# Down projection of a two-layer trunk: Winograd's seven products in another order, their row sums made one layer step earlier

## The chip, the cores and the metric

The kernel runs on one core of a Trainium2 chip. The metric is the device time of one execution in microseconds (us). TensorE (PE) multiplies, VectorE (DVE) and ScalarE (ACT) prepare its operands and empty its accumulators, SyncE (SP) issues all large transfers from one queue in order.

## The reference, cut to what matters

Two layers on 1024 tokens of width 1024. The first mixes tokens by sparse attention, the second by a short gated convolution; each is followed by a feed-forward block of hidden width 2816 and a scaled addition to the residual stream x.

```python
def _swiglu(h, w_gate, w_up, w_down):
    return (jax.nn.silu(h @ w_gate) * (h @ w_up)) @ w_down

def reference(x, c, ...):
    c_act = jax.nn.silu(c)
    for i in range(DEPTH):
        mod = c_act @ ada_w[i] + ada_b[i]
        sh1, sc1, g1, sh2, sc2, g2 = [m[:, None, :] for m in jnp.split(mod, 6, axis=-1)]
        h = _rmsnorm(x, norm1_g[i]) * (1.0 + sc1) + sh1
        ...
        x = x + g1 * y
        h = _rmsnorm(x, norm2_g[i]) * (1.0 + sc2) + sh2
        x = x + g2 * _swiglu(h, ffn_w_gate[i], ffn_w_up[i], ffn_w_down[i])
    return x
```

The change concerns the last product, the down projection `... @ w_down`, and what stands around it.

## The kernel before, in words

Everything is held with the features on the 128 partitions and 512 tokens (one half of the sequence) along the free dimension, so a tile is 128x512 in float32. A float32 product is made of three fast ones: `split` writes a rounded copy `hi` (a CAST on ACT) and the rest `lo` (a subtraction on DVE) of each operand, and `mm3` multiplies hi by hi, hi by lo and lo by hi.

The large products use Winograd's variant of Strassen: both operands are cut into 2x2 blocks, and seven products of sums of blocks take the place of eight. The weights' sums are S1 to S4, the activations' sums are T1 to T4, and M1 to M7 are the products. M1 takes two blocks as they are, M6 takes S2 and T2, M5 takes S1 and T1, M7 takes S3 and T3, M3 takes S4 and one block, M4 takes one block and T4, M2 two blocks.

`Tail` holds the code from the first feed-forward block to the end. It runs `ffn` (layer 0), `down_pairs`, `conv`, `down`, `ffn` (layer 1), `down_pairs`. In `ffn` a set is 256 hidden features: a `Pair` of weight columns for the gate and one for up, seven products each (84 matmuls of 512 columns). `norm_second` forms the second half's operands at the start of `ffn` and of `conv`; meanwhile the first two products of the first `EARLY` = 8 pairs, which need the first half alone, are made (`Pair.early`), and what does not fit is put away in DRAM (`Pair.put`, `Pair.get`). The hidden rows go to DRAM (`hidden`). `side_steps` does eight steps per set of the second layer's modulation, one DVE multiply-add (`adacc`) each.

`down_pairs` sums over 11 steps p of 256 hidden features, and takes four passes over them: M1 and M2 in one, M6 and M5, M7 and M3, and M4 alone. A product of one step is 12 matmuls into four PSUM banks, so a pass of two products holds all eight banks (tags mm, g and sm) and the next pass needs them empty. T1, T2, T3 and T4 are formed by DVE inside the passes from rows that the first pass fetches. In the fourth pass the generator `between` runs the next norm (`norm_first`) or the stores of the output (`store`).

The order on each engine is not written by hand: each operation is recorded, and `Plan.drain` issues them by a cost model, on each engine the earliest recorded of those that are ready. The result is a fixed order on each engine. All instructions are issued from one helper, so that every row of the profile has line L244; tiles tell them apart. In `down_pairs` the tiles named ph hold weights and operands there, rt, rh and cv hold rows, whi and wlo are the operands from the ring of `unit`, u and v are scratch, xr is x, raw are loaded weights.

Of the kernel before, what the change touches and what calls it, by code (L numbers as in the profile page):

```python
# [450 lines left out]
P = 128  # L451
# [900 lines left out]
class Tail:  # L1352
# [4 lines left out]
    EARLY, KEPT, SIDE = 8, 4, 4  # L1357
# [3 lines left out]
    def __init__(self, tk, ada_w, xspill):  # L1361
        self.tk, self.nc, self.plan, self.ada_w = tk, tk.nc, tk.plan, ada_w
        plan = tk.plan
        plan.pri = None
        xp = Pool(plan, "x2")
        self.up = Pool(plan, "u", bufs=6)
        self.bp = Pool(plan, "h2")
        self.tp = Pool(plan, "t2")
        self.sp = Pool(plan, "s2", bufs=4)
        self.first = (xp, self.up, self.bp)  # L1370
        self.second = (self.tp, self.sp)
        xr = xp.tile([P, KT, T], F32, name="xr")
# [3 lines left out]
        self.hid = [[plan.wrap(plan.tc.dram_tile([P, HW], F32, name="hid%d_%d" % (i, f)), [P, HW])  # L1376
                     for f in range(FT)] for i in range(NH)]
# [164 lines left out]
    def down_pairs(self, w, layer, j, between):  # L1542
# [4 lines left out]
        order = range(FT // 2)  # L1547
        hi, raw = (self.bp.tile([P, 8, HW], t, name="p" + v, tag=v)
                   for v, t in zip(self.FIRST, (F32R, F32)))
        b, loads, units = {}, [], []  # L1550
        x = lambda i, k, d: (1 - k, 4 * i + d)

        def rows(p):
            if p in b:
                return b[p]
            if p == 0:
                b[p] = [self.cv() for _ in range(4)]
            else:
                name = self.SECOND[(p - 1) // 2]
                t = self.tp.tile([P, 8, HW], F32, name="r" + name, tag=name)  # L1560
                for i in range(2):
                    b[p + i] = [t.part_of(4 * i + v)[:, 4 * i + v] for v in range(4)]
            return b[p]

        def fetch(p, k):
            for i in range(2):
                nc.sync.dma_start(rows(p)[2 * k + i], self.hid[1 - k][2 * p + i])

        def load(p, half):
            i = len(loads) % 4 * 2  # L1570
            loads.append(raw.part_of(i)[:, i:i + 2])
            nc.sync.dma_start(loads[-1], w[2 * p * P:(2 * p + 2) * P, half_of(half)].rearrange(
                "(j p) n -> p j n", p=P))
            return loads[-1][:, 0], loads[-1][:, 1]
# [6 lines left out]
        def total(x, y, op, s=None):  # L1581
            s = self.s4() if s is None else s
            tt(s, x, y, op)
            return s

        def products(ps, p, *ab):
            for bank, (a, c) in zip(ps, ab):
                (ahi, alo), (chi, clo) = tk.unit(), tk.unit() if len(ps) == 1 else unit()
                self.tk.split(a, ahi, alo)
                self.tk.split(c, chi, clo)  # L1590
                for d in range(4):
                    tk.mm3(bank[d], ahi[:, blk(d)], alo[:, blk(d)], chi, clo,
                           p == order[0], p == order[-1])

        def banks():
            return [[tk.ps("sm") if (i, d) == (0, 3) else self.bank() for d in range(4)]
                    for i in range(2)]

        def add_to(ps, i, k, d):
            self.add(ps, layer, j, *x(i, k, d))  # L1600

        ps = banks()
        for n, p in enumerate(order):
            fetch(p, 0)
            products(ps, p, *zip(load(p, 0), rows(p)[0:2]))
            if n:
                fetch(order[n - 1], 1)
        fetch(order[-1], 1)
        u = [self.u() for _ in range(4)]
        for d in range(4):  # L1610
            self.plan.copy(u[d], ps[0][d])
        for d in range(4):
            add_to(ps[1][d], 0, 0, d)
            add_to(u[d], 0, 0, d)
        ps = banks()
        for p in order:
            b11, b21, b12, b22 = rows(p)
            a21, a22 = load(p, 1)
            s1 = total(a21, a22, add)
            a11 = tk.load(w[blk(2 * p), half_of(0)])  # L1620
            s2 = total(s1, a11, sub)
            t1 = total(b12, b11, sub)
            total(b22, t1, sub, b11)
            products(ps, p, (s2, b11), (s1, t1))
        for d in range(4):
            nc.vector.tensor_tensor(u[d], u[d], ps[0][d], op=add)
        for d in range(4):
            v = self.v()
            nc.vector.tensor_tensor(v, u[d], ps[1][d], op=add)
            add_to(v, 0, 1, d)  # L1630
            add_to(v, 1, 1, d)
            add_to(u[d], 1, 0, d)
        ps = banks()
        for p in order:
            b11, b21, b12, b22 = rows(p)
            (a11, a12), (a21, a22) = (load(p, i) for i in range(2))
            s3 = total(a11, a21, sub)
            t3 = total(b22, b12, sub)
            s4 = total(s3, a22, sub)
            total(s4, a12, add, s4)  # L1640
            products(ps, p, (s3, t3), (s4, b22))
        for d in range(4):
            add_to(ps[0][d], 1, 1, d)
            add_to(ps[0][d], 1, 0, d)
        for d in range(4):
            add_to(ps[1][d], 0, 1, d)
        ps = [[tk.ps("g") for _ in range(4)]]
        for p in order:
            next(between, None)
            b11, b21, b12, b22 = rows(p)  # L1650
            a22 = tk.load(w[blk(2 * p + 1), half_of(1)])
            products(ps, p, (a22, total(b21, b11, sub)))
        for _ in between:
            pass
        for d in range(4):
            add_to(ps[0][d], 1, 0, d)


    def ffn(self, layer, w_gate, w_up):
        sets = [(Pair(self, w_gate, f), Pair(self, w_up, f)) for f in range(0, FF, 2 * P)]  # L1660
        self.norm_second(layer, 1, [p for s in sets for p in s][:self.EARLY])
        for f, (gate, up) in enumerate(sets):
# [6 lines left out]
            for i, row in enumerate(up.done()):  # L1669
# [33 lines left out]
    def run(self, w_gate, w_up, w_down, w_in, w_out, out):  # L1703
        self.side = [(1, j, i, k) for j in range(1, 6) for i in range(NH) for k in range(KT)]
        self.ffn(0, w_gate[0], w_up[0])
        self.down_pairs(w_down[0], 0, 5, self.norm_first(1, 0))
# [3 lines left out]
        self.down_pairs(w_down[1], 1, 5, (self.store(out, half, d) for half, n in ((0, KT), (1, 4))  # L1710
                                          for d in range(n)))
        for d in range(4, KT):
            self.store(out, 1, d)

    def store(self, out, half, d):
        ps, o = self.tk.ps(), self.u()
# [111 lines left out]
```

## Time and profile before

| | |
|---|---|
| time, median of 3 runs | 2344.18 us (2337.61 to 6151.19) |
| the profiled execution | 2345.58 us, span 2343.9 us |
| PE busy | 2262.7 us (97%), 11742 matmuls |
| DVE busy | 1901.5 us (81%) |
| ACT busy | 1109.5 us (47%) |
| moved by DMA | 312.32 MB, 133 GB/s over the span |

The share of the span in which an engine had an instruction in it is averaged over stages. On PE the recorded matmuls overlap, so what it does not do is read from its waits and from the distance of the starts.

### The profile page before, as it was taken

The numbers are of one execution on the slowest core, as the hardware profiler recorded it, in microseconds if no ns is written. First come the engines' busy times: TensorE is split into PE (matmuls) and PEld (weight loads), VectorE is DVE, ScalarE is ACT, GpSimd is POOL, SyncE is SP. The second block draws the span as 40 slices with busy tenths as digits, with TensorE's granted clock in tenths as the row PEclk, the third lists the DMA queues.
The fourth block names the chain that finished last, engine by engine and source line by source line (L and its number), as shares of the span: only waits on it lengthen the run. The fifth ranks groups of instructions, "written<-read, shape, count | busy, mean of one in ns | idle before, by whom it ended". The sixth has DMA issues, their size and how long they took to land.

```text
span 2343.9 us, 32878 instructions
## 1 busy us (share of the span) xinstructions
PE 2262.7 (97%) x11742; PEld 1830.8 (78%) x11742; DVE 1901.5 (81%) x3848; ACT 1109.5 (47%) x2109; POOL 5.6 (0%) x19
## 2 busy tenths in 40 slices
PE   6999999999999999999999899999999999999999
PEld 6657876876797888888887677788878888888877
DVE  6879999777679888878599989886898766666996
ACT  3576899846655333333343552223553333334434
POOL 0000000000000000000000000000000000000000
PEclk7999999999999999999999999999999999999999
DMA  8424243433334554444844144334344322238343
GB/s 286 133 63 89 89 120 95 132 122 104 118 118 139 175 171 135 135 135 138 326 144 151 58 128 126 90 90 157 109 121 146 97 90 77 90 118 313 126 162 113
DMA packets 305134, 312.32 MB, mean 133 GB/s; under 512 B 15145, under 2 KB 209738, under 8 KB 304970
## 3 DMA queue, kind: packets, MB, share of 16 engines
q1 hardware_dynamic: 303530, 308.91, 42.2%
q8 instruction: 92, 1.51, 0.3%
q10 hardware_dynamic: 1440, 1.31, 0.2%
q14 instruction: 72, 0.59, 0.1%
HBM read 259.05 MB, written 51.12 MB: 132 GB/s over the span
## 4 chain that ended last, share of the span: by engine, by line
PE 71%; DVE 15%; issue 7%; DMA 5%; ACT 2%; POOL 0%; SPq 0%; DVEq 0%; ACTq 0%; POOLq 0%
PE ps_g L244 39%; PE ps_mm L244 23%; PE ps_sm L244 5%; DVE u L244 2%; PE ps_L L244 2%; DVE wlo L244 2%; PE ps_o L244 2%; DVE s L244 2%; DVE v L244 2%; DVE p L244 1%; DVE xr L244 1%; DVE sc L244 1%; DMA raw<-in_ffn_w_up_dram 1%; DMA raw<-in_conv_w_in_dram 1%; DMA raw<-in_ffn_w_gate_dram 1%
## 5 line engine op out<-in xcount | busy, mean ns | idle before, releaser
L244 ACT CAST whi<-s 128x512 fp32r<-128x512 f32 x341 | 211.2, 620 | 470.2 <-PE ps_g L244 204.9
L244 PE MATMUL ps_g<-t,whi 128*128 128x512 f32 x1160 | 360.5, 392 | 3.7 <-ACT t L244 3.0
L244 ACT CAST whi<-raw 128x512 fp32r<-128x512 f32 (+1 forms) x283 | 173.0, 618 | 356.6 <-PE ps_g L244 148.4
L244 PE MATMUL ps_g<-h,whi 128*128 128x512 f32 x1080 | 333.7, 390 | 0.0
L244 DVE TENSOR_TENSOR wlo<-raw,whi 128x512 fp32r<-128x512 f32 (+1 forms) x292 | 199.6, 687 | 79.9 <-ACT whi L244 79.3
L244 PEld LDWEIGHTS ps_g<-t,whi 128*128 128x128 f32 x1160 | 218.8, 189 | 51.0 <-ACT t L244 3.4
L244 DVE TENSOR_TENSOR wlo<-s,whi 128x512 fp32r<-128x512 f32 x342 | 234.4, 690 | 23.5 <-ACT whi L244 22.7
L244 PEld LDWEIGHTS ps_g<-h,whi 128*128 128x128 f32 x1080 | 202.1, 188 | 41.5
L244 PE MATMUL ps_g<-t,wlo 128*128 128x512 f32 x580 | 227.4, 392 | 3.9 <-DVE wlo L244 3.9
L244 PE MATMUL ps_g<-h,wlo 128*128 128x512 f32 x540 | 210.6, 390 | 0.3 <-DVE wlo L244 0.3
L244 PE MATMUL ps_g<-ph,whi 128*128 128x512 f32 x660 | 206.5, 392 | 4.2 <-DVE ph L244 2.1
L244 PE MATMUL ps_mm<-t,whi 128*128 128x512 f32 x632 | 197.0, 393 | 3.1 <-ACT whi L244 1.9
L244 PEld LDWEIGHTS ps_g<-ph,whi 128*128 128x128 f32 x660 | 124.9, 189 | 31.2 <-DVE v L244 2.7
L244 PEld LDWEIGHTS ps_mm<-t,whi 128*128 128x128 f32 x632 | 119.8, 190 | 29.2 <-ACT whi L244 2.6
L244 PEld LDWEIGHTS ps_g<-t,wlo 128*128 128x128 f32 x580 | 109.6, 189 | 28.1 <-DVE wlo L244 5.6
L244 PE MATMUL ps_g<-ph,wlo 128*128 128x512 f32 x330 | 129.9, 393 | 0.0
L244 PE MATMUL ps_mm<-t,wlo 128*128 128x512 f32 x316 | 124.2, 393 | 3.3 <-DVE wlo L244 3.3
L244 ACT ACTIVATE p<-p,nm,qsc 128x128 f32<-128x128 f32 (+7 forms) x128 | 112.0, 877 | 27.9 <-DVE nm L244 22.8
L244 DVE CUSTOM_DVE_ANT_0 p<-ps_L,bias 128x512 f32<-128x512 f32 (+3 forms) x192 | 100.1, 553 | 25.3 <-PE ps_sm L244 9.2
L244 PEld LDWEIGHTS ps_g<-h,wlo 128*128 128x128 f32 x540 | 101.4, 188 | 21.9 <-DVE wlo L244 0.8
L244 DVE SCALAR_TENSOR_TENSOR adacc<-adaw,cact,adacc 128x512 f32<-128x512 f32 x140 | 104.8, 748 | 15.6 <-DMA adaw<-in_ada_w_dram 15.3
L244 ACT ACTIVATE junk<-sc,bs 128x896 bf16<-128x896 f32 (+3 forms) x124 | 109.7, 885 | 15.7 <-DVE bs L244 11.1
(334 smaller groups left out, 4738.5 us busy)
## 6 DMA issues: line engine op xcount, KB each, us to landing
ph<-in_ffn_w_down_dram SPq DMA_DIRECT2D x88, 512.0 KB
adaw<-in_ada_w_dram SPq DMA_DIRECT2D x160, 256.0 KB
raw<-in_ffn_w_gate_dram SPq DMA_DIRECT2D x52, 512.0 KB
raw<-in_ffn_w_up_dram SPq DMA_DIRECT2D x52, 512.0 KB
rt<-hid SPq DMA_DIRECT2D x64, 256.0 KB
raw<-in_conv_w_in_dram SPq DMA_DIRECT2D x32, 512.0 KB
hid<-u SPq DMA_DIRECT2D x52, 256.0 KB
raw<-in_ffn_w_down_dram SPq DMA_DIRECT2D x44, 256.0 KB
```

The source lines that it names most:

```text
L244: f(*[a.get() if isinstance(a, Ref) else a for a in args], **{k: a.get() if isinstance(a, Ref) else a for k, a in kw.items()})
```

## The change

It makes T1 to T4 in `ffn`, at the end of each set, and writes seven rows of blocks and sums to DRAM in place of the four hidden rows; `down_pairs` fetches each when a pass needs it. The seven products go in five passes: M1; M6 with M3 one step behind; M5 with M7 one step behind; M2; M4. Each product has four banks, named at each pass. What a finished product adds to x is put on a list and done two entries per step (`later`). `between` runs from the end of the M2 pass on. `EARLY` is 10 in place of 8. One of the five modulation vectors (16 of 80 side steps) moves from the feed-forward block of layer 0 to that of layer 1.

```diff
-    EARLY, KEPT, SIDE = 8, 4, 4
+    EARLY, KEPT, SIDE = 10, 4, 4
...
+        places, loads, units, rest, late = [self.cv() for _ in range(4)], [0], [], [], []
+        for name in ("t4", "t1", "t2", "h22", "t3"):
+            t = self.tp.tile([P, 8, HW], F32, name="r" + name, tag=name)
+            places += [t.part_of(i)[:, i] for i in range(8)]
+        def fetch(p, i, what):
+            nc.sync.dma_start(places[4 * p + i], self.rows[p][what])
...
+        def product(ps, p, a, i, unit=unit):
+            (ahi, alo), (chi, clo) = tk.unit(), unit()
+            tk.split(a, ahi, alo)
+            tk.split(places[4 * p + i], chi, clo)
+            for d in range(4):
+                tk.mm3(ps[d], ahi[:, blk(d)], alo[:, blk(d)], chi, clo, p == 0, p == n - 1)
...
+        def steps(lead, lag=None):
+            for p in range(n):
+                x = lead(p)
+                if late:
+                    f, *a = late.pop()
+                    f(*a)
+                if lag is not None:
+                    late.append((lag, p, x))
+                for f, a in rest[:2]:
+                    f(*a)
+                del rest[:2]
+        def m1(p):
+            fetch(p, 0, "b11")
+            a11, = load(p, 0, 1)
+            product(one, p, a11, 0)
+            fetch(p, 1, "t2")
+        def m6(p):
+            (a11, a12), (a21, a22) = (load(p, i) for i in range(2))
+            tt(a22, a21, a22, add)
+            tt(a22, a22, a11, sub)
+            s4 = self.s4()
+            tt(s4, a12, a22, sub)
+            product(two, p, a22, 1)
+            fetch(p, 2, "b22")
+            fetch(p, 0, "t1")
+            return s4
+        def m3(p, s4):
+            if p == 0:
+                one[:] = banks("g", "g", "g", "sm")
+            product(one, p, s4, 2)
...
+        def m5(p):
+            (a21, a22), (a11,) = load(p, 1), load(p, 0, 1)
+            tt(a22, a21, a22, add)
+            s3 = self.s4()
+            tt(s3, a11, a21, sub)
+            product(two, p, a22, 0)
+            fetch(p, 3, "t3")
+            fetch(p, 1, "b21")
+            return s3
...
+        def m2(p):
+            a12 = tk.load(w[blk(2 * p + 1), half_of(0)])
+            product(two, p, a12, 1, tk.unit)
+            fetch(p, 2, "t4")
+            if p >= start:
+                next(between, None)
+        def m4(p):
+            a22 = tk.load(w[blk(2 * p + 1), half_of(1)])
+            product(one, p, a22, 2, tk.unit)
+            if p >= start - 8:
+                next(between, None)
+        one = banks("g", "g", "g", "sm")
+        steps(m1)
+        u = copies(one, self.u)
+        later(*((add_to, u[d], 0, 0, d) for d in range(4)))
+        two = banks("mm", "g", "mm", "g")
+        steps(m6, m3)
         for d in range(4):
+            nc.vector.tensor_tensor(u[d], u[d], two[d], op=add)
+        later(*((add_to, u[d], 1, 0, d) for d in range(4)))
+        two = banks("mm", "g", "mm", "g")
+        steps(m5, m7)
+        v = copies(two, self.cv)
         for d in range(4):
+            later((tt, v[d], v[d], u[d], add), (add_to, v[d], 0, 1, d), (add_to, v[d], 1, 1, d))
+        two = banks("mm", "g", "mm", "g")
+        steps(m2)
+        add_to(two[0], 0, 0, 0)
+        later(*((add_to, two[d], 0, 0, d) for d in (1, 2, 3)))
+        one = banks("g", "g", "g", "mm")
+        steps(m4)
...
     def ffn(self, layer, w_gate, w_up):
...
-                    self.hidden(2 * f + i, half, t)
+            (b12, b11), (b22, b21) = rows
+            (t2, t1), (t4, _) = gs
+            for t, x, y, op in ((b12, b22, b12, ALU.subtract), (t2, b12, b11, ALU.add),
+                                (t1, b22, t2, ALU.subtract), (t4, b21, t2, ALU.subtract)):
+                self.plan.tt(t, x, y, op)
+            for v, t in (("b11", b11), ("t2", t2), ("b22", b22), ("t1", t1), ("t3", b12),
+                         ("b21", b21), ("t4", t4)):
+                self.nc.sync.dma_start(self.rows[f][v], t)
...
+        self.side = [(1, j, i, k) for j in range(1, 5) for i in range(NH) for k in range(KT)]
         self.ffn(0, w_gate[0], w_up[0])
+        self.down_pairs(w_down[0], 0, 5, self.norm_first(1, 0), 10)
         self.conv(w_in)
         self.down(w_out, KT, 1, 2, self.norm_first(1, 1))
+        self.side = [(1, 5, i, k) for i in range(NH) for k in range(KT)]
         self.ffn(1, w_gate[1], w_up[1])
+        self.down_pairs(w_down[1], 1, 5, (self.store(out, half, d, "sm")
+                                          for half, n in ((0, KT), (1, 4)) for d in range(n)), 8)
         for d in range(4, KT):
+            self.store(out, 1, d, ("g", "mm", "g", "sm")[d - 4])
```

`copies` empties four banks by ACT copies, `load` brings one or two blocks of weights into a ring of eight 128x512 places, `add_to` is `add`, and `m7` is made like `m3`: it empties its banks into four s tiles.

## Rows read from the trace of the kernel before

**Rows 1.** Busy time by stage (us, instructions), TensorE's granted clock, DMA share, GB/s

```profile
690.00:742.00 52.00, 48.57 (x215) 40.01 (x214) 49.69 (x87) 31.85 (x56) 0.00 (x0) 0.97 0.44 127
742.00:854.00 112.00, 110.80 (x499) 91.48 (x499) 95.13 (x159) 35.99 (x63) 0.00 (x0) 1.00 0.57 175
854.00:893.00 39.00, 39.00 (x177) 32.41 (x177) 33.98 (x58) 12.15 (x21) 0.00 (x0) 1.00 0.53 162
1125.00:1248.00 123.00, 123.00 (x546) 101.94 (x546) 98.66 (x160) 53.17 (x93) 0.00 (x0) 1.00 0.58 201
1248.00:1260.00 12.00, 7.83 (x22) 5.52 (x21) 12.00 (x21) 1.44 (x3) 0.00 (x0) 0.72 0.26 81
...
1312.00:1356.00 44.00, 35.54 (x154) 28.78 (x153) 40.81 (x71) 24.98 (x42) 0.00 (x0) 0.92 0.24 73
1401.00:1420.00 19.00, 13.52 (x48) 9.69 (x47) 17.55 (x32) 6.10 (x10) 0.00 (x0) 0.82 0.25 70
1420.00:1530.00 110.00, 109.02 (x475) 88.18 (x474) 100.24 (x177) 27.45 (x46) 0.00 (x0) 1.00 0.35 103
1741.00:1853.00 112.00, 112.00 (x495) 92.75 (x494) 89.70 (x148) 37.00 (x63) 0.00 (x0) 1.00 0.46 140
1853.00:1891.00 38.00, 38.00 (x169) 31.49 (x168) 26.30 (x41) 12.58 (x21) 0.00 (x0) 1.00 0.27 83
```

**Rows 2.** Chain of waits, 1741 to 1830 us: start, length, link

```profile
1749.98 8.16 PE ps_g L244 x36
1758.14 2.72 PE ps_mm L244 x12
```

**Rows 3.** Waits of PE, one stretch after another: total us, times, longest

```profile
PE ps_g L244 <- DVE wlo L244: 3.4, 1, 3.4
...
PE ps_mm L244 <- DVE ph L244: 2.1, 1, 2.1
PE ps_mm L244 <- DVE v L244: 2.1, 1, 2.1
...
PE ps_g L244 <- DVE wlo L244: 8.5, 2, 6.0
...
PE ps_g L244 <- ACT t L244: 3.0, 1, 3.0
PE ps_mm L244 <- ACT whi L244: 1.9, 1, 1.9
...
PE ps_mm L244 <- DVE wlo L244: 3.3, 1, 3.3
...
PE ps_g L244 <- DVE ph L244: 2.1, 1, 2.1
PE ps_g L244 <- DVE v L244: 2.1, 1, 2.1
```

**Rows 4.** Timeline of PE after the second pass: start, length, idle time before

```profile
1252.04 0.50 PE L244 MATMUL ps_mm<-ph,whi 128*128 128x512 f32 x1 [2.08 <-DVE v L244]
1254.63 0.80 PE L244 MATMUL ps_mm<-ph,whi 128*128 128x512 f32 x1 [2.09 <-DVE ph L244]
1255.23 0.63 PE L244 MATMUL ps_mm<-ph,wlo 128*128 128x512 f32 x1
1255.65 0.63 PE L244 MATMUL ps_g<-ph,whi 128*128 128x512 f32 x1
...
1259.92 0.45 PE L244 MATMUL ps_g<-ph,whi 128*128 128x512 f32 x1
```

**Rows 5.** Timeline of DVE there

```profile
1251.30 0.69 DVE L244 TENSOR_TENSOR v<-u,ps_mm 128x512 f32<-128x512 f32 x1
1251.90 0.75 DVE L244 SCALAR_TENSOR_TENSOR xr<-u,mod,xr 128x512 f32<-128x512 f32 x1
1252.56 1.42 DVE L244 SCALAR_TENSOR_TENSOR xr<-v,mod,xr 128x512 f32<-128x512 f32 x2
```

**Rows 6.** Busy time by stage around the start of the first pass

```profile
1120.00:1130.00 10.00, 10.00 (x50) 8.39 (x49) 8.34 (x16) 3.16 (x6) 0.00 (x0) 1.00 1.05 395
1140.00:1150.00 10.00, 10.00 (x46) 8.29 (x45) 5.05 (x8) 3.77 (x7) 0.00 (x0) 1.00 1.05 385
```

More of the change, by code (lines that the diff above doesn't have):

```diff
@@ L1376, in __init__ @@
         self.hid = [[plan.wrap(plan.tc.dram_tile([P, HW], F32, name="hid%d_%d" % (i, f)), [P, HW])
-                     for f in range(FT)] for i in range(NH)]
+                     for f in range(KT)] for i in range(NH)]
+        self.rows = [{v: plan.wrap(plan.tc.dram_tile([P, HW], F32, name="row%d%s" % (f, v)),
+                                   [P, HW]) for v in ("b11", "b21", "b22", "t1", "t2", "t3", "t4")}
+                     for f in range(FT // 2)]
         self.away = [[plan.wrap(plan.tc.dram_tile([P, HW + 2], F32, name="aw%d_%d" % (i, j)),
@@ L1540, in down, with down_pairs, load @@
             self.add(ps, layer, j, 1, d)
-    def down_pairs(self, w, layer, j, between):
+    def down_pairs(self, w, layer, j, between, start):
         tk, nc, tt, add, sub = self.tk, self.nc, self.plan.tt, ALU.add, ALU.subtract
-        order = range(FT // 2)
+        n = FT // 2
         hi, raw = (self.bp.tile([P, 8, HW], t, name="p" + v, tag=v)
                    for v, t in zip(self.FIRST, (F32R, F32)))
[L1550 to L1574, printed above, removed]
+        places, loads, units, rest, late = [self.cv() for _ in range(4)], [0], [], [], []
[4 more added lines that the diff above has]
+            nc.sync.dma_start(places[4 * p + i], self.rows[p][what])
+        def load(p, half, m=2):
+            i = (loads[0] + m - 1) // m * m % 8
+            loads[0] = i + m
+            nc.sync.dma_start(raw.part_of(list(range(i, i + m)))[:, i:i + m],
+                              w[2 * p * P:(2 * p + m) * P, half_of(half)].rearrange(
+                                  "(j p) n -> p j n", p=P))
+            return [raw.part_of(i + k)[:, i + k] for k in range(m)]
         def unit():
@@ L1595, in banks @@
[L1595 to L1609, printed above, removed]
@@ L1610, in down_pairs @@
-        for d in range(4):
-            self.plan.copy(u[d], ps[0][d])
-        for d in range(4):
[L1613 to L1641, printed above, removed]
@@ new lines, in banks, with add_to, later, copies @@
+        def banks(*tags):
+            return [tk.ps(t) for t in tags]
+        def add_to(v, i, k, d):
+            self.add(v, layer, j, 1 - k, 4 * i + d)
+        def later(*calls):
+            rest.extend((f, a) for f, *a in calls)
+        def copies(ps, tile):
+            ts = [tile() for _ in range(4)]
+            for t, v in zip(ts, ps):
+                nc.scalar.copy(t, v)
+            return ts
+        def steps(lead, lag=None):
[9 more added lines that the diff above has]
+                del rest[:2]
@@ new lines, in m7 @@
+        def m7(p, s3):
+            if p == 0:
+                one[:] = banks("g", "g", "g", "sm")
+            product(one, p, s3, 3)
+            if p == n - 1:
+                z = copies(one, self.s4)
+                later(*((add_to, z[d], 1, 1, d) for d in range(4)),
+                      *((add_to, z[d], 1, 0, d) for d in range(4)))
+        def m2(p):
[4 more added lines that the diff above has]
+                next(between, None)
@@ L1655, in down_pairs @@
         for d in range(4):
-            add_to(ps[0][d], 1, 0, d)
+            add_to(one[d], 1, 0, d)
     def ffn(self, layer, w_gate, w_up):
```

36 lines of the change are left out of this document (6 added, 30 removed).

## The prediction

> **What bounds the kernel now.** I read the stages first. From 690 us on PE is busy in nearly every microsecond at a granted clock of 1.00, except in a few short stretches where the clock falls to between 0.72 and 0.97 [rows 1]. Where nothing is in the way it starts a matmul of 512 columns every 0.227 us: 36 of them in 8.16 us, 12 in 2.72 us [rows 2]. The change leaves the matmuls as they are (seven products of 132 per down projection, 924 x 0.227 = 209.5 us), so what it can win is only time in which PE waits. The table of waits then gives the places, and all of them name DVE or ACT, never a DMA [rows 3]. The timeline shows that such a wait costs twice: after two gaps of 2.1 us the starts are 0.42 us apart until 1259.92, and 0.227 us again behind that [rows 4]. The granted clock of that stretch is 0.72 [rows 1], a mixture of full speed and of the half-speed level at 1.2 GHz, which PE had fallen to in the gaps.
>
> The places, each as wait plus some ten matmuls at 0.2 us extra:
> - `norm_second` of layer 0's feed-forward: 3.4 us waited [rows 3], some 5.4 with the clock; of layer 1's: 3.3, some 5.1.
> - Between the second and third pass of `down_pairs`: 2.1 + 2.1 us in either layer [rows 3, 4], some 7.5 in layer 0 and 6.6 in layer 1. DVE is busy 12.00 of 12 us there [rows 1]: it empties eight banks and adds u and v into x one after another [rows 5].
> - In the fourth pass of layer 0, where `norm_first` competes for DVE: 8.5 us in two waits [rows 3], some 10.9.
> - `norm_second` of the convolution: 3.0 + 1.9 us named [rows 3], with smaller waits and the clock some 8.8 (PE's clock is 0.82 over 19 us [rows 1]).
>
> Together 5.4 + 5.1 + 7.5 + 6.6 + 10.9 + 8.8 = 44.3 us. Two per cent of the time, about what a measurement of this kernel can tell from no change, is 47 us. Even without one of these waits the kernel would hardly be faster by that.
>
> **The change, part by part.** A DVE operation on a whole tile starts 0.60 us after the one before it, one with three operands 0.66 us (1251.30, 1251.90, 1252.56 [rows 5]).
>
> *Sums moved.* Per step `down_pairs` loses four DVE sums (T1 to T4), 44 per layer or 44 x 0.60 = 26.5 us, and each set of `ffn` gains four, 2.4 us. Nothing is saved in sum. In `down_pairs` DVE had 98.66 of 123 us busy in the first two passes [rows 1], so relief there shortens only the waits. In `ffn` the cover is PE's own time: a full set has 14 products, 168 x 0.227 = 38.1 us, and in the late sets DVE has room. In the sets whose first products are already made PE needs only 120 x 0.227 = 27.2 us, and there the cover is thin (first rival). I take nothing for the sums on the path.
>
> *Rows in DRAM.* Per layer 77 tiles are written and read in place of 44, 33 x 0.26 MB more each way. M1 and M6 with M3 need six tiles of 0.26 MB per 5.44 us, 1.57 MB or 289 GB/s: M1 a row, a row ahead and a block of weights per 2.72 us, M6 four blocks and two rows per 5.44 us. The first pass before asks the same and is served at 395 and 385 GB/s without any wait of PE [rows 6]. The writes wait in SP's queue for DVE's last sums of the set, and the next pair's weights stand behind them, but the order of that queue already has four such writes per set and PE waits for no load [rows 3]. Value 0; up to +10 us if single loads come late.
>
> The Trainium skill speaks against this part (SBUF — State Buffer, The DMA setup-cost knee): a transfer pays a fixed cost, so that one of 256 KiB reaches 224 GB/s and one of 1 MiB 341, and small ones should be joined. By that a step of M6 would take 1.57 MB / 224 GB/s = 7.0 us in place of 5.44. The trace does not agree for a deep queue: stretches that move mostly 256 KB rows run at 385 to 395 GB/s [rows 6].
>
> *Passes of one product in flight.* M1 holds four banks, M6 the other four, and M3 takes M1's a step later. While DVE or ACT empties four banks (4 x 0.60 to 0.66 = 2.6 us) PE has a lagging product of the pass before, 2.72 us, or two. The additions into x come two per step (1.3 us of a 5.44 us step in which seven sums and splits take 4.2 us). So the wait between the second and third pass should go: -7.5 and -6.6. New hand-overs (four per layer) are bounded by nothing, as at the start of the first pass now, and by one such stall each; I take +3 us for all.
>
> *`norm_first` earlier and longer.* It starts at the end of the M2 pass, and M4's step has two splits in place of two and a sum. Over M4's 29.9 us and M2's last step DVE then has 22 x 0.60 + 15 adds and shifts of the norm's 23 whole-tile operations at 0.60 to 0.66 (some 14.5 us in all) + 4 x 0.66 = about 30 us for some 32.6 us of PE, where it had 42 (33 operations at 0.60, the norm, twelve additions into x) for 29.9. The two waits of 8.5 us should nearly go; I take -8 of 10.9 (between 0 and -10.9).
>
> *Ten early products.* Two more pairs begun are 4 x 2.72 = 10.9 us of work for PE during `norm_second`, at six more DVE operations there, 3.6 us. A wait of 3.4 us plus 3.6 us of delay is less than 10.9 us, so the wait goes in each of three places, unless DVE is the limit for long after it. In layer 0 DVE is at 95.13 of the next 112 us [rows 1], and it gets the new sums on top: I take -3 of 5.4. The convolution has DVE at 100.24 of 110 us after that stall [rows 1]: -5 of 8.8. Layer 1 gets 16 side steps (16 x 0.66 = 10.6 us of DVE) at just this place: -2 of 5.1; at worst +6. Layer 0 loses the same steps late, where they cost nothing.
>
> *The end.* One store fewer after M4, other tags for the banks: -1.
>
> Sum: -7.5 - 6.6 + 3 - 8 - 3 - 5 - 2 - 1 = -30.1. The profiled execution took 2345.58 us, 1.4 above the median 2344.18 and 1.7 above its span, so 2345.6 - 30 = 2315.5; I say 2315.
>
> **The rivals.**
>
> *DVE becomes the bound of the early sets (slower side).* With ten early pairs the first five sets of `ffn` take PE 136 us; they get 20 sums, 12.1 us, and must also make up the wait that is gone. Layer 0 has 151 - 95.1 - 34.0 = 21.9 us of idle DVE there [rows 1] for 12.1 + 5.4 = 17.5. Layer 1 has 150 - 89.7 - 26.3 = 34.0 us for 12.1 + 5.1 + 10.6 = 27.8. It fits only if more than four fifths of the idle time can be used. If none could, PE would wait 12.1 + 22.7 us, and the 5 us that I count in these places would be lost: 2315 + 5 + 34.8 = 2355, slower than now. If half can, some 2327. For it: DVE's many waits for PE results there are not all fillable. Against it: PE does not wait once from 1741 to 1891 us at 77% of DVE. Chance of the full case 0.10.
>
> *The hand-overs stall all the same.* The emptying is the same work, and a bank that DVE frees late stops PE for about 7 us with the clock, as it does now. If two of four per layer do, 4 x 7 - 3 = +25: 2340. For it: it does so today. Against it: the start of the first pass, which also needs all banks, does not. Chance 0.13.
>
> *Transfers bind.* If the queue fell below 289 GB/s, M1 and M6 would go at its pace. At the mean of the first two passes, 201 GB/s [rows 1], a step takes 7.8 us, 2.4 more; over M1 (5.5 such steps) and M6 (11) in two layers 79 us: 2394. But 201 is what was asked for, and 385 what was given [rows 6]. Chance 0.04. (The rule of the Trainium skill cited above points to this case.)
>
> *All waits go.* 2345.6 - 44.3 - 1 = 2300. Needs DVE to have no queue at the norms. Chance 0.10.
>
> *It does not do what it says.* The planner fixes the order by its own costs; if the lagging products were not placed into the gaps, the case is that of the stalled hand-overs.
>
> **How the numbers follow.** The forecast, 2305 to 2327, has a chance of 0.63, with the half case of the first rival in it; the full one 0.10, stalled hand-overs 0.13, transfers 0.04, all waits gone 0.10. From 2300 to 2342 the range takes in the forecast, the hand-overs and half of the last case, and leaves out some 0.19. Faster by over 2% (below 2297) needs more than all the waits: 0.04. Slower by over 2% (above 2391) only the transfers at their worst, 0.02. Within 2%: 0.94.
>
> **What would show it.** No wait of PE by DVE of 2 us between the M6 and M5 passes, and a clock of 1.00 there; DVE near 75% in `down_pairs` and up by four operations of 0.60 us per set in `ffn`; the wait near the end of `norm_second` gone or below 2 us; `norm_first` without the 6 us wait. The prediction is wrong if PE waits after `norm_second` for whi or wlo in sets one to four (first rival), at a bank just emptied (second), or for raw, or for rows from DRAM, in M1 and M6 (third).

## The result, and the profile after

| | before | after |
|---|---|---|
| median of 4 runs each | 2341.8 us (2337.61 to 6151.19) | 2309.88 us (2305.7 to 2314.05) |
| ratio, 95% interval | | 0.987, 0.9837 to 0.9902 |
| profiled execution, span | 2345.58, 2343.9 us | 2312.89, 2311.2 us |
| PE busy | 2262.7 us (97%) | 2256.3 us (98%), 11742 matmuls |
| DVE busy | 1901.5 us (81%) | 1894.6 us (82%) |
| moved by DMA | 312.32 MB | 356.39 MB |

The kernel is faster by 1.3%, which is less than the 2% by which a change is called faster here. The interval keeps it apart from no change all the same. The run of 6151.19 us is left out of the ratio, but not of the median of before; without it that median is 2339.42 us, and the two medians are 29.5 us apart.

The stages can be cut at matmuls that both kernels have: the first product of a feed-forward block reads h, the first of a down projection reads ph, the out projection's reads rh. These lines are answers for single instructions on PE, of the kernel after (start, length, engine, line, operation, output and operands):

```profile
683.77 0.40 PE L244 MATMUL ps_g<-h,whi 128*128 128x512 f32 x1
1120.35 0.61 PE L244 MATMUL ps_g<-ph,whi 128*128 128x512 f32 x2
1332.83 0.39 PE L244 MATMUL ps_g<-h,whi 128*128 128x512 f32 x1
1619.72 0.39 PE L244 MATMUL ps_g<-rh,whi 128*128 128x512 f32 x1
1665.59 0.39 PE L244 MATMUL ps_g<-h,whi 128*128 128x512 f32 x1
2088.22 0.39 PE L244 MATMUL ps_g<-ph,whi 128*128 128x512 f32 x1
```

In the kernel before the same six stand at 688.41, 1125.51, 1355.68, 1642.53, 1688.35 and 2114.29 us. The differences of neighbours, with the span as the last end, give the stages, us. Below the two kernels stand the experiments of the next section. "Rest" is the span less the head, the part ahead of the feed-forward block of layer 0. The change does not touch the head, but it differs by up to 8.6 us from one execution to another, so the rest compares better than the span. A single stage has a spread of its own: e9 is the changed kernel once more, and its convolution took 284.4 us in place of 286.9; the last stage, which no run from e6 to e10 edits, took from 223.0 to 225.3. A difference of some 2.5 us in one stage of one execution shows nothing by itself.

| | head | ffn 0 | down 0 | conv | out proj. | ffn 1 | down 1 and end | rest |
|---|---|---|---|---|---|---|---|---|
| before | 688.4 | 437.1 | 230.2 | 286.8 | 45.8 | 425.9 | 229.6 | 1655.5 |
| after | 683.8 | 436.6 | 212.5 | 286.9 | 45.9 | 422.6 | 222.9 | 1627.4 |
| e1_early8 | 684.9 | 433.8 | 211.6 | 291.3 | 45.8 | 427.7 | 222.8 | 1632.9 |
| e2_no_stagger | 683.3 | 437.3 | 211.6 | 286.7 | 45.8 | 422.6 | 222.6 | 1626.6 |
| e3_sums_back | 686.6 | 430.3 | 217.2 | 284.7 | 45.7 | 422.6 | 227.5 | 1628.1 |
| e4_sums_only | 684.7 | 435.5 | 228.9 | 288.9 | 45.9 | 427.6 | 229.5 | 1656.3 |
| e5_early10_only | 682.0 | 430.9 | 231.3 | 281.3 | 45.7 | 420.8 | 229.3 | 1639.3 |
| e6_no_sums | 683.9 | 432.6 | 212.0 | 284.0 | 45.9 | 422.7 | 224.4 | 1621.5 |
| e7_late_ada | 686.1 | 431.2 | 212.4 | 282.9 | 45.7 | 422.6 | 224.1 | 1618.9 |
| e8_conv_one_tap | 690.6 | 435.2 | 211.8 | 280.0 | 45.5 | 422.6 | 225.3 | 1620.4 |
| e9_change_again | 687.2 | 437.1 | 212.4 | 284.4 | 45.9 | 422.6 | 223.0 | 1625.4 |
| e10_late_again | 682.4 | 431.0 | 212.2 | 283.3 | 45.6 | 422.6 | 224.1 | 1618.8 |
| e11_order_only | 685.0 | 434.6 | 215.2 | 289.6 | 45.6 | 428.0 | 225.5 | 1638.4 |
| e12_adds_at_once | 686.5 | 434.6 | 215.6 | 285.9 | 45.8 | 422.6 | 224.9 | 1629.5 |

Of the 32.7 us between the two spans 4.6 lie in the head, so the change is worth 28.1 us: 17.7 in the first down projection, 6.7 in the second, 3.3 in the feed-forward block of layer 1, and almost nothing in that of layer 0 and in the convolution.

Busy time by stage after, with the columns of [rows 1]: stretch and its length, PE, PE's weight loads, DVE, ACT, POOL, granted clock, DMA share, GB/s. The stages behind the first down projection start 23 to 26 us earlier than before, so the same times are not the same work there.

```profile
740.00:852.00 112.00, 111.44 (x498) 91.50 (x496) 98.43 (x165) 35.11 (x61) 0.00 (x0) 1.00 0.64 198
852.00:891.00 39.00, 35.86 (x150) 29.27 (x150) 36.32 (x62) 10.21 (x18) 0.00 (x0) 0.91 0.58 182
1120.00:1150.00 30.00, 30.00 (x134) 24.85 (x133) 20.32 (x33) 12.91 (x23) 0.00 (x0) 1.00 1.05 391
1150.00:1210.00 60.00, 59.72 (x262) 48.79 (x262) 54.23 (x88) 27.65 (x47) 0.00 (x0) 1.00 1.00 365
1150.00:1330.00 180.00, 179.66 (x798) 148.08 (x798) 156.77 (x256) 90.08 (x156) 0.00 (x0) 1.00 0.54 189
1333.00:1420.00 87.00, 86.81 (x388) 71.21 (x388) 80.60 (x142) 42.58 (x76) 0.00 (x0) 1.00 0.52 150
1420.00:1530.00 110.00, 106.38 (x452) 85.02 (x451) 99.15 (x172) 26.50 (x44) 0.00 (x0) 0.98 0.36 105
1530.00:1619.00 89.00, 86.92 (x375) 71.21 (x375) 61.24 (x103) 30.87 (x54) 0.00 (x0) 0.98 0.44 138
1744.00:1856.00 112.00, 112.00 (x504) 92.96 (x503) 100.11 (x165) 37.20 (x64) 0.00 (x0) 1.00 0.58 181
```

The clock tells most. Between the passes of the first down projection it was 0.72, near its end 0.92 [rows 1]. Now it is 1.00 from 1150 to 1330 us, and PE is busy in 179.66 of 180. The dip has not left the feed-forward block of layer 0, it has moved: 0.91 from 852 to 891 us, where before it was 1.00. In the convolution PE is busy in 86.81 of the first 87 us now, and 3.6 us of PE are missing from 1420 to 1530 and 2.1 behind that. The first 64 us of that stage before were:

```profile
1356.00:1420.00 64.00, 58.52 (x254) 47.21 (x253) 59.45 (x105) 33.95 (x60) 0.00 (x0) 0.95 0.42 119
```

The waits of PE after, in the stretches where there is any of 1 us or more (what waits, for whom: total us, times, longest), are to be held against [rows 3]. The first two are from 840 to 1000 us, the others from 1333 to 1619:

```profile
PE ps_sm L244 <- DVE adacc L244: 2.8, 2, 2.6
PE ps_g L244 <- DVE wlo L244: 0.9, 3, 0.4
...
PE ps_g L244 <- ACT whi L244: 2.3, 2, 2.1
PE ps_mm L244 <- ACT whi L244: 1.6, 1, 1.6
PE ps_mm L244 <- DVE wlo L244: 1.5, 1, 1.5
```

From 1200 to 1333 us and from 1660 us to the end no wait of PE is listed. The waits after `norm_second` (3.4 and 3.3 us in the feed-forward blocks, 3.0 and 1.9 in the convolution), those of 2.1 us between the passes and the 8.5 us of the fourth pass are gone. What came in their place is small: one wait of 2.6 us for adacc, and three of 1.5 to 2.1 us in the convolution.

### The profile page after: what moved, and what is told of

It reads as the page before. It is cut to its first block, busy times and chain, and to the rows that moved or that the text cites. A ratio compares the mean times of both kernels' runs of the same rounds, so it can differ in the third digit from the quotient of the medians.

```text
span 2311.2 us, 33159 instructions
## 1 busy us (share of the span) xinstructions
PE 2256.3 (98%) x11742; PEld 1825.8 (79%) x11742; DVE 1894.6 (82%) x3842; ACT 1119.9 (48%) x2131; POOL 5.6 (0%) x19
## 2 busy tenths in 40 slices
DMA packets 334192, 356.39 MB, mean 154 GB/s; under 512 B 18089, under 2 KB 218826, under 8 KB 334026
## 4 chain that ended last, share of the span: by engine, by line
PE 52%; DVE 5%; DMA 3%; issue 1%; ACT 0%; ACTq 0%; SPq 0%; DVEq 0%
PE ps_g L244 35%; PE ps_mm L244 14%; PE ps_sm L244 3%; DMA raw<-in_conv_w_in_dram 2%; DVE u L244 1%; DVE v L244 1%; DVE wlo L244 1%; DVE s L244 1%; DMA ph<-in_ffn_w_down_dram 1%; DVE t L244 0%; ACT whi L244 0%; DVE cv L244 0%; DMA adaw<-in_ada_w_dram 0%; DMA row10t<-cv 0%; DMA s<-hid 0%
## 5 line engine op out<-in xcount | busy, mean ns | idle before, releaser
L244 ACT CAST whi<-raw 128x512 fp32r<-128x512 f32 (+1 forms) x305 | 186.6, 618 | 385.6 <-PE ps_g L244 146.4
L244 ACT CAST whi<-s 128x512 fp32r<-128x512 f32 x276 | 170.7, 620 | 354.9 <-PE ps_g L244 159.4
L244 PE MATMUL ps_g<-h,whi 128*128 128x512 f32 x1056 | 328.0, 392 | 0.0
L244 DVE TENSOR_TENSOR wlo<-raw,whi 128x512 fp32r<-128x512 f32 (+1 forms) x314 | 214.7, 688 | 89.8 <-ACT whi L244 89.2
L244 DVE TENSOR_TENSOR wlo<-s,whi 128x512 fp32r<-128x512 f32 x276 | 189.5, 689 | 16.9 <-ACT whi L244 15.9
L244 PE MATMUL ps_mm<-t,whi 128*128 128x512 f32 x608 | 189.1, 392 | 1.7 <-ACT whi L244 1.6
L244 PE MATMUL ps_g<-ph,whi 128*128 128x512 f32 x572 | 176.6, 389 | 0.0
L244 PEld LDWEIGHTS ps_g<-ph,whi 128*128 128x128 f32 x572 | 107.4, 188 | 22.3
L244 PE MATMUL ps_mm<-t,wlo 128*128 128x512 f32 x304 | 119.0, 392 | 0.0
L244 DVE TENSOR_TENSOR u<-u 128x512 f32<-128x512 f32 x170 | 114.9, 689 | 1.8 <-ACT u L244 0.8
```

Source lines behind the costliest of these rows:

```text
L244: f(*[a.get() if isinstance(a, Ref) else a for a in args], **{k: a.get() if isinstance(a, Ref) else a for k, a in kw.items()})
```

## The experiments

The theory was that of the prediction: the gain comes from passes with one product in flight, which PE does not have to wait for, and from the ten early products. The rivals were that the sums moved into `ffn` make the gain, or take part of it back, and that one of the smaller edits (stagger, additions one by one) carries it.

**Ten early products.** First the changed kernel with eight:

```diff
-    EARLY, KEPT, SIDE = 10, 4, 4
+    EARLY, KEPT, SIDE = 8, 4, 4
```

> The changed kernel with 8 early products in place of 10. Theory A (the wait at the end of norm_second that the ten remove is given back soon after, because VectorE stays the limit for long): the stages of layer 0's feed-forward and of the convolution keep their length within 2 us (436.6 us and, with the out projection, 332.8), the one of layer 1's feed-forward grows by some 3 us; in all +3 us, 2313. Theory B (each of the three waits of 3 to 6 us is worth what it costs): +5, +9 and +5 us, in all +19, 2329.

Measured: 2319.23 us, 0.9903 (0.9881 to 0.9925) of before. The rest is 5.5 us longer than after. The sign differs by stage: the convolution is 4.4 us longer and the feed-forward block of layer 1 5.1, where the wait after `norm_second` is back (2.5 us for wlo), but that of layer 0 is 2.8 us shorter, although PE waits there for wlo after `norm_second` again (3.4 us); the wait for adacc is not there. Neither theory holds: the time lies between the two, and the convolution is longer than theory A has it, layer 0's block shorter than either. Then the kernel before with ten:

```diff
-    EARLY, KEPT, SIDE = 8, 4, 4
+    EARLY, KEPT, SIDE = 10, 4, 4
```

> The kernel before with 10 early products in place of 8 and nothing else. If the ten bring the same by themselves as they did inside the change (9 us), the convolution stage falls by 4 us (286.8 to 282) and layer 1's feed-forward by 5 (425.9 to 421), layer 0's by 0 to 5 (its VectorE has no new sums here), in all -9 to -14, 2329. If the down projections' new order is what lets them pay, under 4 us.

Measured: 2328.97 us, 0.9949 (0.9929 to 0.9969), 11 us faster. Here all three places gain, 6.2, 5.5 and 5.1 us. So the wait goes in each of them, and in the changed kernel something takes it back in layer 0 and in the convolution.

**The stagger.** M3 and M7 are made in the step of their partner in place of one step later:

```diff
-                if late:
-                    f, *a = late.pop()
-                    f(*a)
                 if lag is not None:
-                    late.append((lag, p, x))
+                    lag(p, x)
```

> The changed kernel with M3 and M7 recorded in the same step as M6 and M5, not one step behind. Theory A (four banks per product do it, and the planner fills the gaps with whatever product is ready): the down projections stay within 2 us of 212.5 and 223.0 us, time within 4 us of the changed kernel. Rival (the lagging product is what covers the emptying of the banks): two hand-overs per layer with a wait of 2 to 3 us and the lost clock each, 5 us x 4 = +20 us, with waits of PE by VectorE at the start of M5 and M2.

Measured: 2310.74 us, 0.9867 (0.9838 to 0.9896). No stage is more than 0.9 us from the changed kernel's. The step of delay brings nothing. Theory A puts the gain on the four banks of each product; no run takes those away by themselves.

**The sums back in the down projection.** The new order and the new banks stay, but T1 to T4 are formed by DVE in the passes from the four hidden rows, five sums per step and layer, and `ffn` makes none (cut to M6 and the end of `ffn`):

```diff
-            product(two, p, a22, 1)
-            fetch(p, 2, "b22")
-            fetch(p, 0, "t1")
+            b11, b21, b12, b22 = places[4 * p:4 * p + 4]
+            t1 = self.s4()
+            tt(t1, b12, b11, sub)
+            tt(b11, b22, t1, sub)
+            product(two, p, a22, 0)
+            fetch(p, 1, "b21")
...
-                self.plan.tt(t, x, y, op)
...
+                    self.hidden(2 * f + i, half, t)
```

> The changed kernel with the order of products kept, but T1 to T4 made in the down projection from four rows in DRAM, as before (five sums per step, T1 being made twice), and none in the feed-forward layer. Theory A (the order and the banks bring most of it): the down projection of layer 0 takes some 215 us, of layer 1 224, with only the M4 pass of layer 0, where the norm needs VectorE, 2 to 4 us longer; layer 0's feed-forward 4 us shorter; in all 0 to +3 us. Rival (the relief of VectorE brings it): 225 and 228 us, in all +15.

Measured: 2311.64 us, 0.9877 (0.9854 to 0.9901), and a rest 0.7 us from the changed kernel's. The sums moved into `ffn` cost about what they save: without the move it is 4.7 and 4.6 us more in the down projections, 6.3 less in the feed-forward block of layer 0, and 2.2 less in the convolution, which is within the spread of that stage. Then the reverse, the kernel before with the sums in `ffn`, rows from DRAM, and the old four passes (e4). The same edit of `ffn` as in the change; in the passes a row is fetched in place of each sum:

```diff
-            fetch(p, 0)
+            fetch(p, p0="b11", p1="b21")
...
-            products(ps, p, (a22, total(b21, b11, sub)))
+            products(ps, p, (a22, t4))
```

> The kernel before, with its four passes, eight early products and its banks, but T1 to T4 made in the feed-forward layer and fetched. Theory A: the wait between the second and third pass stays (20 additions and emptyings in a row), so layer 1's down projection takes 228 us or more and layer 0's some 222, since the norm's wait in the fourth pass shrinks; in all -5 to -9 us against before, 2334. Rival: both down projections come near those of the changed kernel (213 and 223), in all -22 us.

Measured: 2342.74 us, 1.0006 (0.9993 to 1.002). Alone the sums bring nothing, neither the 5 to 9 us of theory A nor the 22 of the rival; the first down projection took 228.9 us, not 222. Waits of PE from 1225 to 1365 us in this kernel, in the form of [rows 3]:

```profile
PE ps_g L244 <- DVE wlo L244: 7.5, 2, 5.0
PE ps_mm L244 <- DVE v L244: 2.1, 1, 2.1
PE ps_mm L244 <- DVE ph L244: 1.9, 1, 1.9
```

They are about those of before, 8.5, 2.1 and 2.1 us, though DVE has one sum less in each step of the fourth pass. Last, the order alone (e3 with eight early products, so that neither the sums nor `EARLY` are changed from before):

```diff
-    EARLY, KEPT, SIDE = 10, 4, 4
+    EARLY, KEPT, SIDE = 8, 4, 4
```

> The new order of the products alone: the kernel with T1 to T4 made in the down projection, and 8 early products. If the parts add up, it lacks what the ten early products bring (11 us when alone) and has the rest: feed-forward of layer 0 437 us, down projections 217 and 227.5, convolution 290, feed-forward of layer 1 428; time 2324, ratio 0.993. If the order needs the earlier start of the next stage to pay, 2330 or more.

Measured: 2324.08 us, 0.9918 (0.99 to 0.9937), 16 us faster than before, which is the sum that was expected if the parts add up. Its first down projection, by stage, to be held against the line of the same stretch of after:

```profile
1150.00:1330.00 180.00, 178.51 (x787) 145.40 (x786) 178.54 (x298) 92.60 (x159) 0.00 (x0) 1.00 0.40 134
```

DVE is busy in 178.54 of 180 us, and PE still has 178.51 and a clock of 1.00. So the hand-overs are freed by the new order and what comes with it, not by fewer sums. What comes with it is all that is left of the change: the banks, the emptying of M1, M5 and M7 by ACT copies, the additions two per step, `between` from the end of the M2 pass on, and the modulation vector moved to layer 1. Taken alone this group is worth 16 us and the early products 11; together 27, and e3, which has both, measured 29.

The moved vector shows in the feed-forward blocks: against before that of layer 0 is 2.5 us shorter in e11 and that of layer 1 2.1 longer. With the vector go two row sums on PE, of some 0.8 us each (eight matmuls of one column, from 1776.27 to 1777.07 us in the changed kernel), which would make up most of it.

**The additions into x spread out.** `later` executes them at once:

```diff
         def later(*calls):
-            rest.extend((f, a) for f, *a in calls)
+            for f, *a in calls:
+                f(*a)
```

> The changed kernel with the additions into x recorded all at once where a product ends, not two per step. Theory banks (only four banks have to be empty, and PE has a product in the other four meanwhile): the hand-overs stay without a wait over 1 us, the down projections at 212.5 and 223 us. Rival (what stopped PE between the second and third pass was the row of twenty VectorE operations, and it is their spreading that removed the wait): after M5 and M7 now 20 operations, some 13 us, stand in a row again, PE waits there 3 to 5 us and runs at half clock for as long, each down projection 5 to 8 us longer, the time 2322.

Measured: 2315.88 us, 0.9879 (0.9863 to 0.9896), which can't be told from the changed kernel in total. The first down projection is 3.1 us longer, with 2.6 us of waits for wlo early in the M2 pass, the longest 1.7. The second is 2.0 us longer, which is within the spread of that stage, and its longest wait is 0.7 us. So the waits of 3 to 5 us of the rival do not come. Spreading is worth up to some 5 us, the smaller part of the 24.4 that the down projections win.

**What takes the gain back in layer 0.** The dip at 852 to 891 us is opened by the timeline of PE in the changed kernel (start, length, idle time before):

```profile
883.90 1.84 PE L244 MATMUL ps_sm<-ones,adacc 128*128 128x1 f32 x8 [2.61 <-DVE adacc L244]
885.60 1.20 PE L244 MATMUL ps_g<-h,whi 128*128 128x512 f32 x2
886.59 0.63 PE L244 MATMUL ps_g<-h,wlo 128*128 128x512 f32 x1
887.02 1.05 PE L244 MATMUL ps_g<-h,whi 128*128 128x512 f32 x2
...
890.79 0.39 PE L244 MATMUL ps_g<-h,whi 128*128 128x512 f32 x1
```

Eight matmuls of one column sum a modulation vector (adacc) over the partitions. They need the last side step, and PE, which works in its fixed order, waits 2.61 us for it with large products queued behind. Then it is at half speed for some 5 us, starts 0.42 us apart. Why the side step is late is seen on ACT and DVE at the same time:

```profile
879.32 1.15 ACT L244 CAST whi<-raw 128x512 fp32r<-128x512 f32 x2 [3.08 <-DMA raw<-in_ffn_w_gate_dram]
879.98 1.29 DVE L244 TENSOR_TENSOR wlo<-raw,whi 128x512 fp32r<-128x512 f32 x2 [1.52 <-ACT whi L244]
881.74 0.75 DVE L244 SCALAR_TENSOR_TENSOR adacc<-adaw,cact,adacc 128x512 f32<-128x512 f32 x1 [0.47 <-DMA adaw<-in_ada_w_dram]
882.41 0.68 DVE L244 TENSOR_TENSOR v<-v,ps_g 128x512 f32<-128x512 f32 x1
883.00 0.75 DVE L244 SCALAR_TENSOR_TENSOR adacc<-adaw,cact,adacc 128x512 f32<-128x512 f32 x1
```

and in SP's queue (start, length of issue, queue):

```profile
875.05 1.00 SPq L244 DMA_DIRECT2D raw<-in_ffn_w_gate_dram  x2
876.17 7.93 SPq L244 DMA_DIRECT2D adaw<-in_ada_w_dram  x4
```

DVE first stands 1.52 us for ACT, which had waited 3.08 us for a load of raw. The loads of the modulation weights (adaw, two places) follow each other in the single queue over 7.93 us, and DVE waits 0.47 us for one of them, in the side step ahead of the last. The queue in turn waits for DVE to free the places of adaw (12.4 us in all from 830 to 900). So DVE and the queue hold each other up, and these rows do not show which of them is the cause. Two runs go further. The first leaves out the four sums of each set of `ffn` (the rows are written all the same, with what the tiles hold):

```diff
-            for t, x, y, op in ((b12, b22, b12, ALU.subtract), (t2, b12, b11, ALU.add),
-                                (t1, b22, t2, ALU.subtract), (t4, b21, t2, ALU.subtract)):
-                self.plan.tt(t, x, y, op)
```

> The changed kernel without the four sums per set in the feed-forward layers; the seven rows are written and fetched all the same, so four of the seven products get rows that are not summed. Theory V (VectorE is the bound of layer 0's sets one to four): layer 0's feed-forward falls from 436.6 to 430 us, as where the sums were put back, the convolution stays, layer 1's stays at 422.6. Rival Q (the matmul that adds up the modulation, placed in PE's fixed order, waits for a weight load late in SP's queue): with the same transfers it stays at 434 us or more.

Measured, in one execution: 2307.12 us, and a feed-forward block of layer 0 of 432.6 us, 4.0 less than after. That lies between the 430 and the 434 of the two theories. The wait for adacc is gone with the same transfers, so the queue alone does not make it: DVE, with four operations less per set, is in time. From 740 to 891 us, first the changed kernel, then this one:

```profile
740.00:891.00 151.00, 147.31 (x647) 120.77 (x646) 134.75 (x226) 45.32 (x79) 0.00 (x0) 0.98 0.62 194
```

```profile
740.00:891.00 151.00, 148.20 (x664) 121.61 (x663) 126.68 (x211) 46.91 (x82) 0.00 (x0) 1.00 0.64 199
```

The second keeps the sums and moves only the row sum, half a set later:

```diff
         if k == KT - 1:
-            tk.ada_end(layer, j, [self.acc], half)
+            self.ends.append((layer, j, [self.acc], half))
...
     def side_steps(self):
+        if self.ends:
+            tk_end = self.ends.pop(0)
+            self.tk.ada_end(*tk_end)
```

> The changed kernel with the small matmuls that end a modulation vector recorded half a set (some 19 us) later. Theory Q (PE waits there for adacc 2.6 us and then runs at half clock, 5.7 us in all): layer 0's feed-forward falls from 436.6 to 431 us and the time to 2305. Theory V (VectorE is the bound): the wait only moves to a product's wlo, 435 us or more, time unchanged.

Measured: 2306.1 us, 0.9847 (0.983 to 0.9863), and 431.2 us in that block, 5.4 less than after with all the sums in place. To see whether this holds, the changed kernel and this one were run once more, side by side on one chip:

> The changed kernel once more, to stand on the same chip and in the same rounds as the next one. If all that differs between executions is the stage before 690 us, which no part of the change touches: stages as before (436.6, 212.5, 286.9, 45.9, 422.6, 222.9) within 1 us each, ratio 0.987.

> The changed kernel with the ends of the modulation vectors half a set later, once more, beside the changed kernel. Theory Q (the wait for adacc is the place where layer 0 gave back what the ten early products won): 4 us or more below the changed kernel, at 431 us in layer 0's feed-forward. Rival (the first comparison was the spread between executions): within 2 us of it.

Measured: 2312.89 us, 0.9874 (0.9855 to 0.9893), and 2305.41 us, 0.9844 (0.9828 to 0.9859). The four runs of the one lie between 2309.35 and 2315.47, those of the other between 2302.9 and 2306.07, so they do not overlap. The block is 437.1 and 431.0 us, and all that PE waits in the second from 684 to 1110 us is

```profile
PE ps_g L244 <- DVE wlo L244: 2.0, 2, 1.2
```

Of the stages of the changed kernel, expected within 1 us each, the convolution was 2.5 us shorter this time. The version with the later row sum beats both kernels: it is 34.9 us under the median of before on that chip (2340.32 us), the changed kernel 27.4.

**What takes it back in the convolution.** In the changed kernel two of the three taps are left out, 32 operations of DVE with three operands:

```diff
-                    for j in (1, 2):
+                    for j in ():
```

> The changed kernel with one of the three taps of the convolution: 32 VectorE operations of 0.66 us, 21 us, are left out. If VectorE bounds the convolution's first sets, where the ten early products gave back what they won, PE's waits there (1470, 1490 us) go and the stage falls from 286.9 to 281 us. Rival (the loads of raw, of which there are two places, come too late for SP's order): the waits of ACT for raw stay and the stage stays above 285.

Measured, in one execution: 2312.76 us with a long head of 690.6; the convolution is 280.0 us, 6.9 less than after and 4.4 less than in e9. By stage, against the line for 1420 to 1530 us of after:

```profile
1420.00:1530.00 110.00, 110.00 (x487) 91.09 (x487) 93.32 (x166) 28.69 (x48) 0.00 (x0) 1.00 0.41 122
```

PE is full when DVE has less to do, and no wait of PE is listed from 1345 to 1545 us. So DVE sets the pace of the convolution's first sets. One of the two waits that went, 1.6 us for whi, had stood behind a load of raw; that DVE frees the places of raw too late for these loads fits, but was not shown apart. The wait near the end of the stage stays. All that PE waits in this stage of e8 is

```profile
PE ps_g L244 <- ACT whi L244: 3.5, 2, 2.5
```

The 2.5 us come behind 5.28 us in which ACT waits for a row from DRAM, as the 2.1 us of after come behind 4.86. This third wait of the convolution is thus a different one, and no run tests what sets it.

## Why the prediction was right, and where it was not

The forecast was -30.1 us on the profiled execution. The stages that the change touches gave -28.1, the spans -32.7, because 4.6 us of the shorter head came by luck. The median 2309.88 us lies 5 us under the forecast 2315, because the forecast started from a profiled execution 6.2 us above the median of the other runs of before (2339.42). The sum is right partly because two errors cancel: the down projections gave 24.4 us where 20.1 were expected, the early products 3.7 where it was 10. (924 x 0.227 is 209.7, not 209.5; nothing rests on it.)

**Hand-overs: -7.5, -6.6 and +3; `norm_first`: -8; the end: -1.** These are the down projections, -14.0 in layer 0 (-7.5 - 8 + 1.5) and -6.1 in layer 1 (-6.6 + 1.5 - 1) with the +3 halved. Measured: -17.7 and -6.7. The waits go as said, and the +3 for new hand-overs did not come: no wait of PE over 0.3 us is left in either down projection. The falls are near the whole price of the old waits in the prediction, 7.5 + 10.9 = 18.4 and 6.6, so the -8 for `norm_first` was too small. The reason given was in part wrong: relief for DVE by the moved sums was not needed for this, as e11 shows, in which no wait over 0.7 us is left in the first down projection at 178.54 of 180 us of DVE; its two down projections are together 5.3 us longer than the changed kernel's. Of the sign of DVE near 75% the second down projection gave 73% (162.57 of 222.8 us), the first, where the norm is made too, 84% (178.57 of 212.45). Here the advice of the Trainium skill (Perfetto Trace Analysis, Optimizing Tensor Performance) to let independent groups rotate through the PSUM banks, so that emptying one overlaps the products of the next, agrees with the runs: the group of order and banks, without the sums, gave 0.9918. Which part of that group frees the hand-overs and which the norm (four banks each, the emptying by ACT, the earlier start of the norm) was not separated; the stagger is out, and the spreading is the smaller part.

**Sums moved: nothing on the path.** Right as a net, wrong in its parts: 9.3 us are won in the down projections (e3 against after) and 6.3 lost in the feed-forward block of layer 0. The first rival named the place, the early sets of layer 0, but its price of 35 us was far off and its way was another one. PE loses little through operands of large products that are late there (0.9 us for wlo in three waits). It loses through one row sum of the side work in its queue, at 5.4 to 6.1 us. The step that failed is the sentence that the cover of the sums in the early sets is PE's own time, with 21.9 us of idle DVE for 17.5: the balance of DVE held over the stretch, but DVE's order did not hold the time of one operation on which PE's order relied. That the balance held is seen in e10, which has all the sums: with the row sum later the block takes 431.0 us, with 2.0 us of waits. In layer 1 the same sums cost nothing: with them and without (e3) that block takes 422.6 us, and PE is busy throughout (422.60 us, clock 1.00).

**Ten early products: -3, -5, -2.** Alone they are worth -6.2, -5.5 and -5.1 (e5), in the feed-forward blocks as much as the wait with its half-speed stretch (5.4 and 5.1 by the prediction), in the convolution less (8.8). In the change -0.5, +0.1 and -3.3 is what is left to the whole stage, in order of layer 0, convolution, layer 1. Layer 0 lost its share to the row sum. Layer 1 has the two row sums of the moved vector, some 1.6 us of PE that the prediction did not count. The convolution is the term that was mis-sized: its -5 was taken although DVE had 100.24 of 110 us after the stall [rows 1]. The wait after `norm_second` did go, 86.81 of 87 us from 1333 us on in place of 58.52 of 64, but PE waits later: 1.5 and 1.6 us near 1470 and 1490, where e8 shows that DVE is the limit, and 2.1 us at 1607, behind a row from DRAM. Kernels with eight early products take 288.9 to 291.3 us in the convolution (e1, e4, e11) where before took 286.8. One of them, e4, has the old order, so it is not shown that the gain of the new order is given back there.

**Rows in DRAM: 0.** Right. M1 and M6 moved 391 and 365 GB/s where 289 were needed, and PE waits for no load there (59.72 of 60 us busy in M6). The estimate of 7.0 us for a step of M6, from the fixed cost of a transfer in the Trainium skill (SBUF — State Buffer, The DMA setup-cost knee), did not hold for this queue. It also took all six tiles as transfers of 256 KB; the four blocks of weights came as two of 512 KB. The traffic grew by 44.07 MB, not only by the 34.6 MB of the rows: with ten early products 12 more tiles are put away and fetched again and six more loads of 512 KB made, which the prediction did not list.

**Left open.** Two executions of the changed kernel differ by 2.5 us in the convolution, 286.9 and 284.4 (e9). The lines of the whole stage, first after, then e9, show where it lies:

```profile
1332.83:1619.72 286.89, 281.00 (x1217) 228.17 (x1216) 241.88 (x417) 100.81 (x175) 0.00 (x0) 0.99 0.43 129
1336.67:1621.11 284.44, 276.84 (x1217) 226.13 (x1216) 242.11 (x417) 101.35 (x175) 0.00 (x0) 1.00 0.43 130
```

PE waits more in the second (7.6 us against 5.6), but its granted clock stays at 1.00, where it is 0.99 in the first. Why the clock fell in one of them only is not known. In e4 it is open why the fourth pass still waits 7.5 us with a sum less per step. Whether rows could be kept in SBUF to save DRAM traffic was not tried.

## What to carry to other kernels

When the full engine stops at the change of a pass because all banks must be emptied, give each product half of the banks and let another product run meanwhile; here that held with VectorE busy in 178.54 of 180 us, and moving its work elsewhere added nothing. Count a wait of TensorE with the stretch at half speed behind it, and look in its fixed order for tiny instructions of a side computation: one that stands at the point where its operand is just ready cost 5.4 to 6.1 us here, and standing half a set later it waited for nothing. The same edit, ten early products, was worth 5.5 us in the convolution by itself and nothing inside the change, so compare by stages and not by the total alone.

## What the runs showed of the hardware that was not expected

- A row sum of eight matmuls on one column each, which waited 2.61 us and took 1.84, cost 5.4 to 6.1 us with the half-speed stretch behind it.
- 391 GB/s over 30 us and then 365 over 60 us were moved while PE was busy in 89.72 of 90 us, in transfers of 256 KB and, from 1118 to 1210 us, 25 of 512 KB.
- The head, which no edit touches, took from 682.0 to 690.6 us in fourteen profiled executions, as much as several of the effects looked for here.
